# Attention with negated scores: one pass per head over local and context scores, value halves summed by TensorE

## Chip, cores and metric

One core of one Trainium2 chip runs the whole program. The metric is the device time of one execution in microseconds (us), the median over the runs shown. Engines: TensorE (PE, its weight loads PEld), VectorE (DVE), ScalarE (ACT), GpSimd (POOL), and SyncE (SP), which issues most DMAs.

## The reference, cut to the attention

The program is two transformer blocks on 1024 tokens of width 1024. The change lies in the attention of the first block. Half of the heads ("a", 8 heads on 2 key heads, with a sink column) look at a window of three 128-token blocks, the others ("b", 8 heads) at a neighbourhood with a learned bias; all look at 256 context tokens as well.

```
s_loc = einsum(q, k_local) * scale        # + bias for b
s_loc = where(mask, s_loc, -inf)
s_ctx = einsum(q, k_ctx) * scale
p = softmax(concat([s_loc, s_ctx, sink_col]))   # sink only for a
o = p_loc @ v_local + p_ctx @ v_ctx
```

## The kernel before, in words

The attention runs over 64 units: 32 of kind a, then 32 of kind b. A unit `(kind, i, p)` is one block of 128 queries (`i` = 0 to 7) and one pair of heads (`p` = 0 to 3; the two heads are `e` = 0, 1). A unit has three local key tiles of 128 (two where `i` is 0 or 7) and two context tiles, so 640 or 512 scores per query and head. Products are made exact to nearly fp32 by splitting one operand into a high and a low part in the type `fp32r`, so that a unit's scores take two matmuls for each piece (`z` = 0, 1), and its values are stacked with their low parts ("halves"), which have to be added at the end.

The steps of a unit `x`:

- `f_s(x, e)`: TensorE writes local scores into a tile `ps_l` (a PSUM bank, two of them) and context scores into `ps_c` (one bank for both heads).
- `f_max(x, e)`: VectorE reads `ps_l`, adds mask or bias, writes `sp` in SBUF and leaves the row maximum in `m` (one custom instruction and one that reads the accumulator). `f_maxc(x)`: the same for the context scores of both heads, with a column of zeros as addend, then the maximum of the two maxima (line 964) and its negation (line 968 for a, with the sink; line 971 for b).
- `f_exp(x, e)`: ScalarE computes the exponential with the negated maximum as bias, and the row sum.
- `f_pt(x, gi)`, `gi` = 0, 1, 2: TensorE transposes up to four 128x128 blocks of `sp` into a tile `pp` (a PSUM bank, three in rotation). For `gi` = 0 (the context blocks) ScalarE copies to `pf` and POOL makes high part (line 1003, a multiplication by ones) and low part (line 1004). For `gi` = 1, 2 ScalarE makes the high part (line 1006) and VectorE the low part (line 1007) straight from `pp`.
- `f_pv(x, part)`: the product with the values; ScalarE copies the result to `oT`.
- `f_fin(x)`: TensorE transposes the 128x128 blocks of `oT` (two for a, four for b) into a bank of their own (`otp`), and VectorE's reduction (line 1043) adds the halves while it copies to `O`.

The order is written by hand. Every engine takes its instructions in program order; there is no scheduler. Iteration `n` of the loop issues, in this order:

```
f_s(n,0) f_max(n,0)  f_exp(n-1,0)  f_pt(n-2,0)
f_s(n,1) f_max(n,1)  f_maxc(n)     f_exp(n-1,1)  f_pt(n-2,1)
f_pv(n-3,0)  f_pt(n-2,2)  f_pv(n-3,1)  f_fin(n-4)
conv_q(n//2+1) if n is even, then extra[n]
```

`conv_q` turns the queries of two units (four transposes into a `pp` tile, split by ScalarE, line 898, and VectorE, line 899). `extra[n]` holds work for later: the next head pair's keys (`b_k`, through `pp`), values (`b_v`, POOL) and bias (`b_bias`, one plain fp32 matmul into `pp` and six VectorE additions), the row sums (`a_end`, `b_end`), and splits of coming weights (`W.tick`).

Of the kernel before, what the change touches and what calls it, by code (L numbers as in the profile page):

```python
# [9 lines left out]
F32 = mybir.dt.float32  # L10
# [8 lines left out]
P = 128  # L19
# [193 lines left out]
def kernel(ctx: ExitStack, tc: tile.TileContext, a: dict, out: bass.AP, dbg=None):  # L213
# [219 lines left out]
    for i in (0, 2):  # L433
        nc.gpsimd.tensor_scalar(out=qg[:, i, :], in0=qg[:, i, :], scalar1=0.125, scalar2=None, op0=ALU.mult)
    nc.gpsimd.tensor_scalar(out=nsink, in0=sink, scalar1=-1.0, scalar2=None, op0=ALU.mult)
# [417 lines left out]
    maskA = wk.tile([P, 384], F32, name="maskA")  # L853
    maskB = wk.tile([P, 16, 24], F32, name="maskB")
# [53 lines left out]

    def addend(u, e):
        i = u[1]  # L910
        if u[0] == "a":
            return maskA[:, (128 if i == 0 else 0):(256 if i == 7 else 384)]
        p = u[2]
        if i == 0:
            return B["bE", p][:, e, 1:3].rearrange("p s r c -> p (s r c)")
        if i == 7:
            return B["bE", p][:, e, 0:2].rearrange("p s r c -> p (s r c)")
        return B["bI", p][:, e].rearrange("p s r c -> p (s r c)")

# [11 lines left out]
    def f_s(x, e):  # L931
        u = units[x]
        kk = kt(u[1])
        nl = len(kk) * P
        if e == 0:
            st["c", x] = ps_c.tile([P, 512], F32, tag="sc", name="ps_c", bufs=1)
        pc = st["c", x]
        pl = ps_l.tile([P, 512], F32, tag="sl", name="ps_l", bufs=2)
        k = k_stack(u, e)
        for z in range(2):  # L940
            q = qhl[x // 2][z][:, 2 * (x % 2) + e]
            nc.tensor.matmul(pl[:, 0:nl], q, k[:, kk[0] * P:kk[0] * P + nl], start=(z == 0), stop=(z == 1))
            nc.tensor.matmul(pc[:, e * 256:e * 256 + 256], q, k[:, 1024:1280], start=(z == 0), stop=(z == 1))
        st["l", x, e] = pl

    def f_max(x, e):
        u = units[x]
        if e == 0:
            st["sp", x] = wk.tile([P, 2, 640], F32, tag="sp", name="sp", bufs=3)
            st["m", x] = wk.tile([P, 8], F32, tag="m", name="m", bufs=4)  # L950
        nl = len(kt(u[1])) * P
        nc.vector.tensor_tensor_reduce(
            out=st["sp", x][:, e, 0:nl], in0=st.pop(("l", x, e))[:, 0:nl], in1=addend(u, e), scale=1.0, scalar=NEG,
            op0=ALU.add, op1=ALU.max, accum_out=st["m", x][:, e:e + 1])

    def f_maxc(x):
        u = units[x]
        nl = len(kt(u[1])) * P
        sp, m, pc = st["sp", x], st.pop(("m", x)), st.pop(("c", x))
        for e in range(2):  # L960
# [4 lines left out]
        nm, sm = stat(u)  # L965
        if u[0] == "a":
            h0 = 2 * u[2]
# [4 lines left out]
        st["nm", x] = (nm, sm)  # L972

    def f_exp(x, e):
        u = units[x]
        nm, sm = st["nm", x]
        sp = st["sp", x]
        w = len(kt(u[1])) * P + 256
        nc.scalar.activation(out=sp[:, e, :w], in_=sp[:, e, :w], func=AF.Exp, bias=nm[:, e:e + 1],
                             accum_out=sm[:, e:e + 1])  # L980

    def f_pt(x, gi):
        u = units[x]
        nk = len(kt(u[1])) + 2
        nl = nk - 2
# [12 lines left out]
        ph, pl = pt[:, g[0]:g[0] + len(g), 0, :], pt[:, g[0]:g[0] + len(g), 1, :]  # L998
        pv = pp[:, :w].rearrange("p (b t) -> p b t", t=P)
        if gi == 0:  # L1000
            pf = wk.tile([P, 4, P], F32, tag="pf", name="pf", bufs=2)
            nc.scalar.activation(out=pf, in_=pv, func=AF.Copy)
            nc.gpsimd.tensor_tensor(out=ph, in0=pf, in1=ones.unsqueeze(1).broadcast_to([P, 4, P]), op=ALU.mult)
            nc.gpsimd.tensor_tensor(out=pl, in0=pf, in1=ph.bitcast(F32), op=ALU.subtract)
        else:
            nc.scalar.activation(out=ph, in_=pv, func=AF.Copy)
            nc.vector.tensor_tensor(out=pl, in0=pv, in1=ph.bitcast(F32), op=ALU.subtract)

    def f_pv(x, part):
        u = units[x]  # L1010
        tiles = kt(u[1]) + [8, 9]
        nt_ = len(tiles)
        pt = st["pt", x]
# [3 lines left out]
        if u[0] == "a":  # L1017
            for j in (range(nt_ - 2) if part == 0 else range(nt_ - 2, nt_)):
                for z in range(2):
                    nc.tensor.matmul(po[:, 0:256], v_stack(u, 0, tiles[j]), pt[:, 2 * j:2 * j + 2, z, :],  # L1020
                                     start=(j == 0 and z == 0), stop=(j == nt_ - 1 and z == 1))
        else:
            e = part
            for j, tt in enumerate(tiles):
                nc.tensor.matmul(po[:, e * 256:e * 256 + 256], v_stack(u, e, tt),
# [8 lines left out]

    def f_fin(x):
        kind, i, p = units[x]
        oT = st.pop(("oT", x))
        nb = 2 if kind == "a" else 4
        po = ps_q.tile([P, 512], F32, tag="tq", name="otp")
        for j in range(nb):  # L1040
            tr(po[:, j * P:(j + 1) * P], oT[:, j * P:(j + 1) * P], ident)
        od = O[0 if kind == "a" else 1][:, i, p * 128:p * 128 + 128].rearrange("p (h d) -> p h d", d=64)
# [66 lines left out]
    def b_bias(p, e):  # L1109
        if e == 0:  # L1110
            B["bI", p] = BP[p % 2].tile([P, 2, 3, 16, 8], F32, tag="bI", name="bI")
            B["bE", p] = BP[p % 2].tile([P, 2, 3, 16, 8], F32, tag="bE", name="bE")
# [51 lines left out]
    for t, n in ((maskB, "mask_b"), (maskR, "mask_r"), (jrev, "jrev")):  # L1164
        nc.sync.dma_start(out=t, in_=a[n])
    maskP = wk.tile([P, 2, 640], F32, tag="sp", name="maskP", bufs=3)[:, 0, 0:384]
    load_natural(maskP, a["mask_a"])
    nc.gpsimd.tensor_copy(out=maskA.rearrange("p (b s c) -> p b s c", s=8, c=8),
                          in_=maskP.rearrange("p (b c s) -> p b s c", s=8, c=8))
    for g0 in (8, 0, 4):  # L1170
# [7 lines left out]
    for n in range(NU + 5):  # L1178
# [9 lines left out]
        if ok(n):  # L1188
            f_s(n, 1)
            f_max(n, 1)  # L1190
            f_maxc(n)
        if ok(n - 1):
# [1008 lines left out]
```

## Time and profile before

| what | value |
|---|---|
| median of 3 runs | 2707.81 us (2707.66 to 2713.16) |
| the profiled execution's own time | 2706.59 us |
| its span in the trace | 2704.8 us |
| mean granted clock of TensorE | 0.989 of full |
| busy over the whole span | PE 2569.5 us (95%), DVE 1713.1 (63%), ACT 1060.6 (39%), POOL 1187.3 (44%) |
| first and last of VectorE's score passes | 318.0 us and 638.1 us from the span's start |

The shares of the whole span are means over stages with different limits; the attention is about an eighth of it, and has to be read by itself. The time of a PE row is longer than the distance to the next row, since matmuls overlap; busy time of the weight loads (PEld) is nearer to the time in which TensorE really had work.

### The profile page before, as it was taken

Reading aid. Unit: us, or ns where it says so; the run is one execution under the profiler, and the core shown is the slowest. Engines: PE = TensorE matmul, PEld = TensorE weight load, DVE = VectorE, ACT = ScalarE, POOL = GpSimd, SP = SyncE. Lnnn points to the kernel's source line nnn. Section 1 sums busy time; section 2 is a strip of 40 time slices with the busy share of each in tenths; the row PEclk is TensorE's granted clock in tenths of the full one; section 3 lists DMA queues with packets and bytes.
Section 4 is the critical chain, followed back from the end, with each engine's and each line's share of the span. In section 5 each row is a group of like instructions: output and inputs, shape, how many; then the busy total and the mean of one; then the engine's idle time right before and its main releaser. Section 6 shows DMA issues by size and latency. Waiting matters only on the chain. (4 is left out here: it accounts for less than half of the span.)

```text
span 2704.8 us, 37053 instructions
## 1 busy us (share of the span) xinstructions
PE 2569.5 (95%) x13861; PEld 2135.2 (79%) x13861; DVE 1713.1 (63%) x3361; ACT 1060.6 (39%) x2613; POOL 1187.3 (44%) x1071
## 2 busy tenths in 40 slices
PE   7999888888989999999999999999999999999998
PEld 3999887778977888888878878877777777777786
DVE  4688699997276555555564532421777777777766
ACT  4644487776132222222223533322433333333333
POOL 2355266675256666666653221112333333333321
PEclk9999999999999999999999999999999999999999
DMA  6166421322111111111111111110111111111112
GB/s 241 32 191 205 139 52 34 87 52 87 32 40 32 62 48 47 47 47 48 62 52 51 50 35 44 32 47 32 40 47 47 47 47 47 47 47 47 47 47 86
DMA packets 152541, 170.86 MB, mean 63 GB/s; under 512 B 39444, under 2 KB 135460, under 8 KB 151336
## 3 DMA queue, kind: packets, MB, share of 16 engines
q1 hardware_dynamic: 152200, 168.35, 19.6%
q8 instruction: 109, 1.79, 0.3%
q0 software_dynamic: 160, 0.14, 0.1%
q14 instruction: 72, 0.59, 0.1%
HBM read 154.81 MB, written 13.65 MB: 62 GB/s over the span
## 5 line engine op out<-in xcount | busy, mean ns | idle before, releaser
L140 POOL TENSOR_TENSOR wlo<-raw,whi 128x512 fp32r<-128x512 f32 x132 | 179.2, 1362 | 448.2 <-ACT whi L139 419.3
L1656 PE MATMUL pgu<-h,whi 128*128 128x512 f32 x864 | 342.5, 396 | 3.1 <-DVE h L1592 3.1
L1657 PE MATMUL pgu<-h,wlo 128*128 128x512 f32 x864 | 341.2, 395 | 0.5 <-POOL wlo L140 0.5
L1655 PE MATMUL pgu<-h,whi 128*128 128x512 f32 x864 | 341.3, 395 | 0.0
L140 DVE TENSOR_TENSOR wlo<-raw,whi 128x512 fp32r<-128x512 f32 (+2 forms) x304 | 229.6, 768 | 154.0 <-ACT whi L139 153.3
L139 ACT ACTIVATE whi<-raw 128x512 fp32r<-128x512 f32 (+1 forms) x436 | 232.5, 552 | 173.0 <-DMA raw<-in_w_down 61.1
L1674 DVE TENSOR_TENSOR uv<-pgu,uv 128x512 f32<-128x512 f32 x216 | 148.4, 687 | 149.5 <-PE pgu L1657 128.2
L237 PE MATMUL pdn<-wlo,hid 128*128 128x512 f32 x576 | 227.3, 395 | 12.5 <-DVE wlo L140 12.5
L236 PE MATMUL pdn<-whi,hid 128*128 128x512 f32 x576 | 226.4, 393 | 1.4 <-DVE uv L1383 1.1
L238 PE MATMUL pdn<-whi,hid 128*128 128x512 f32 x576 | 226.6, 393 | 0.0
L1384 POOL TENSOR_TENSOR x<-x,uv 128x512 f32<-128x512 f32 x144 | 192.2, 1359 | 31.5 <-DVE uv L1383 28.6
L1656 PEld LDWEIGHTS pgu<-h,whi 128*128 128x128 f32 x864 | 162.2, 188 | 42.3 <-DVE h L1592 3.6
L1655 PEld LDWEIGHTS pgu<-h,whi 128*128 128x128 f32 x864 | 162.5, 188 | 40.1
L1657 PEld LDWEIGHTS pgu<-h,wlo 128*128 128x128 f32 x864 | 162.2, 188 | 39.9 <-POOL wlo L140 0.9
L1525 POOL TENSOR_TENSOR hid<-sg,hid 128x512 fp32r<-128x512 f32 x80 | 107.1, 1343 | 193.6 <-ACT hid L1524 191.5
L1677 POOL TENSOR_TENSOR uv<-uv 128x512 f32<-128x512 f32 x72 | 106.7, 1481 | 163.6 <-DVE uv L1674 163.6
L236 PE MATMUL pin<-whi,h 128*128 128x256 f32 x512 | 146.1, 285 | 5.8 <-ACT hsq L634 2.1
L237 PE MATMUL pin<-wlo,h 128*128 128x256 f32 x512 | 146.1, 285 | 1.7 <-DVE wlo L140 1.7
L238 PE MATMUL pin<-whi,h 128*128 128x256 f32 x512 | 146.1, 285 | 0.2 <-DVE h L706 0.2
L237 PEld LDWEIGHTS pdn<-wlo,hid 128*128 128x128 f32 x576 | 108.1, 188 | 42.0 <-DVE wlo L140 17.6
L1524 ACT ACTIVATE hid<-sg 128x512 fp32r<-128x512 f32 x80 | 50.3, 632 | 231.6 <-DVE sg L1522 231.6
L236 PEld LDWEIGHTS pdn<-whi,hid 128*128 128x128 f32 x576 | 108.2, 188 | 27.9 <-DVE uv L1383 1.5
(387 smaller groups left out, 7101.7 us busy)
## 6 DMA issues: line engine op xcount, KB each, us to landing
raw<-in_ffn_w_up SPq DMA_DIRECT2D x22, 1024.0 KB
mraw<-in_w_mod SPq DMA_DIRECT2D x32, 512.0 KB
raw<-in_w_gate SPq DMA_DIRECT2D x11, 1024.0 KB
raw<-in_w_up SPq DMA_DIRECT2D x11, 1024.0 KB
raw<-in_w_down SPq DMA_DIRECT2D x11, 1024.0 KB
raw<-in_ffn_w_down SPq DMA_DIRECT2D x11, 1024.0 KB
raw<-in_w_in SPq DMA_DIRECT2D x9, 1024.0 KB
wm<-in_w_mod SPq DMA_DIRECT2D x8, 1024.0 KB
```

The lines of the kernel that those rows point to most:

```text
L139: nc.scalar.activation(out=hi, in_=src, func=AF.Copy)
L140: (engine or self.engine or nc.vector).tensor_tensor(out=lo, in0=src, in1=hi.bitcast(F32), op=ALU.subtract)
L236: nc.tensor.matmul(ps, lh, rh, start=(i == 0), stop=False)
L237: nc.tensor.matmul(ps, lh, rl, start=False, stop=False)
L238: nc.tensor.matmul(ps, ll, rh, start=False, stop=(i == n - 1))
L1384: nc.gpsimd.tensor_tensor(out=xs, in0=xs, in1=tmp, op=ALU.add)
L1525: nc.gpsimd.tensor_tensor(out=hl[:, c], in0=sg[:, cc, c], in1=hh[:, c].bitcast(F32), op=ALU.subtract)
L1655: nc.tensor.matmul(ps, lh, rh, start=start and k == 0, stop=False)
L1656: nc.tensor.matmul(ps, lh, rl, start=False, stop=False)
L1657: nc.tensor.matmul(ps, ll, rh, start=False, stop=stop and k == n - 1)
L1674: nc.vector.tensor_tensor(out=o, in0=ps, in1=u, op=ALU.add)
L1677: nc.gpsimd.tensor_tensor(out=o, in0=u, in1=v, op=ALU.add)
```

## The change

1. The query gains are scaled by -0.125 instead of 0.125, and mask, bias matrix and bias masks are negated once, at the start of the stage (four small POOL instructions and a memset there). All scores are then negated, and the least of them is the bias that `f_exp` needs; `f_exp` takes `scale=-1.0`.
2. Local and context scores of a head lie side by side in one tile `ps_s` of two banks (two tiles, so four banks). `maskA` grows to 896 columns (zeros, mask, zeros), the bias `bI` to 1024 (bias of head 0, zeros, bias of head 1), so that one instruction can add over all 640 scores and leave the least. `f_maxc` is gone. The starting value of the minimum is the negated sink for a (a column read per partition). Only the units of b with `i` = 0 or 7 keep two passes, the second starting from the first's result.
3. For some units context comes ahead of local (`order`). The `pp` groups of `f_pt` are now the tiles in order, so POOL's share (`gi` = 0) is the first four blocks instead of the context blocks.
4. `f_fin` adds the halves by matmuls with `twice`, an identity of 64 columns over an identity of 64 columns (two plain fp32 matmuls of 64 columns for a, four for b), into a `pp` tile; the bank of `otp` is gone. VectorE only copies 128x128.
5. POOL's two multiplications by ones become `tensor_copy`.

```
-    ps_l = pool("ps_l", space=PSUM, stack=st_ps)
-    ps_c = pool("ps_c", space=PSUM, stack=st_ps)
+    ps_s = pool("ps_s", space=PSUM, stack=st_ps)
...
-    ps_q = pool("ps_q", space=PSUM, stack=st_ps)
...
+        ps = ps_s.tile([P, 1024], F32, tag="s", name="ps_s", bufs=2)[:, a0:a0 + w]
+        lo, co = (256, 0) if c1 else (0, nl)
...
+            nc.tensor.matmul(ps[:, lo:lo + nl], q, k[:, kk[0] * P:kk[0] * P + nl], start=(z == 0), stop=(z == 1))
+            nc.tensor.matmul(ps[:, co:co + 256], q, k[:, 1024:1280], start=(z == 0), stop=(z == 1))
...
+        at0 = nsink[:, 2 * u[2] + e:2 * u[2] + e + 1] if u[0] == "a" else -NEG
+        for c0, n, in1 in addends(u, e):
             nc.vector.tensor_tensor_reduce(
-                out=sp[:, e, nl:nl + 256], in0=pc[:, e * 256:e * 256 + 256], in1=zeros, scale=1.0, scalar=NEG,
-                op0=ALU.add, op1=ALU.max, accum_out=m[:, 2 + e:3 + e])
-        nc.vector.tensor_tensor(out=m[:, 4:6], in0=m[:, 0:2], in1=m[:, 2:4], op=ALU.max)
...
-            nc.vector.scalar_tensor_tensor(out=nm, in0=m[:, 4:6], scalar=-1.0, in1=nsink[:, h0:h0 + 2],
-                                           op0=ALU.mult, op1=ALU.min)
-        else:
-            nc.vector.tensor_scalar(out=nm, in0=m[:, 4:6], scalar1=-1.0, scalar2=None, op0=ALU.mult)
+                out=st["sp", x][:, e, c0:c0 + n], in0=ps[:, c0:c0 + n], in1=in1, scale=1.0, scalar=at0,
+                op0=ALU.add, op1=ALU.min, accum_out=nm)
+            at0 = nm
...
-        g = [list(range(2 * nl, 2 * nk)), list(range(0, 4)), list(range(4, 2 * nl))][gi]
+        g = list(range(4 * gi, min(4 * gi + 4, 2 * nk)))
...
-            nc.gpsimd.tensor_tensor(out=ph, in0=pf, in1=ones.unsqueeze(1).broadcast_to([P, 4, P]), op=ALU.mult)
+            nc.gpsimd.tensor_copy(out=ph, in_=pf)
...
-        nb = 2 if kind == "a" else 4
-        po = ps_q.tile([P, 512], F32, tag="tq", name="otp")
-        for j in range(nb):
-            tr(po[:, j * P:(j + 1) * P], oT[:, j * P:(j + 1) * P], ident)
...
-        nc.vector.tensor_reduce(
-            out=od, in_=po[:, :nb * P].rearrange("p (h x d) -> p h d x", h=2, d=64), axis=AX.X, op=ALU.add)
+        nb = 1 if kind == "a" else 2
+        po = pp_tile()
+        for e in range(2):
+            for j in range(nb):
+                b = (nb * e + j) * P
+                nc.tensor.matmul(po[:, e * 64:e * 64 + 64], oT[:, b:b + P], twice, start=(j == 0), stop=(j == nb - 1))
+        nc.vector.tensor_copy(out=O[0 if kind == "a" else 1][:, i, p * 128:p * 128 + 128], in_=po[:, 0:128])
```

What it does to the order of two engines is seen best in one unit. VectorE in an a unit with three local tiles, from its score passes to the last step of `f_fin`, before (`ISA` with 128x1 is the read of the accumulator; `stat` holds the negated maximum):

```order
L952 ISA sp,m<-ps_l,maskA 128x384 [waits PE_49]
L952 ISA m 128x1
L952 ISA sp,m<-ps_l,maskA 128x384 [waits PE_49]
L952 ISA m 128x1
L961 ISA sp,m<-ps_c,zero_3969 128x256 [waits PE_49]
L961 ISA m 128x1
L961 ISA sp,m<-ps_c,zero_3969 128x256
L961 ISA m 128x1
L964 TENSOR_TENSOR m<-m 128x2 [waits DVE_49]
L968 SCALAR_TENSOR_TENSOR stat<-m,nsink 128x2 [waits DVE_49]
L1007 TENSOR_TENSOR pt<-pp,pt 128x4x128 [waits Activation_49,Pool_49]
L1043 TENSOR_REDUCE o_3966<-otp 128x128 [waits PE_49]
```

and of the change:

```order
L961 ISA sp,stat<-ps_s,maskA,nsink 128x640 [waits PE_49]
L961 ISA stat 128x1
L961 ISA sp,stat<-ps_s,maskA,nsink 128x640 [waits PE_49]
L961 ISA stat 128x1
L998 TENSOR_TENSOR pt<-pp,pt 128x4x128 [waits Activation_49,Pool_49]
L998 TENSOR_TENSOR pt<-pp,pt 128x2x128 [waits Activation_49]
L1036 COPY o_3966<-pp 128x128 [waits PE_49]
```

Four passes became two, the two small instructions are gone, and the first low-part subtraction follows the passes directly. TensorE in an a unit, from the second group of transposes to the next unit's scores, before:

```order
L241 MATMUL pp<-ident,sp 128x128 [waits DVE_49]
L241 MATMUL pp<-ident,sp 128x128 x3
L1020 MATMUL po<-pt,VA 128x256 [waits Activation_49]
L1020 MATMUL po<-pt,VA 128x256 x5
L241 MATMUL pp<-ident,sp 128x128 [waits Activation_49]
L241 MATMUL pp<-ident,sp 128x128
L1020 MATMUL po<-pt,VA 128x256 [waits Pool_49] x2
L1020 MATMUL po<-pt,VA 128x256 x2
L241 MATMUL otp<-ident,oT 128x128 x2
L942 MATMUL ps_l<-kstA_4001,q_5648 128x384 [waits DVE_49]
```

and of the change:

```order
L241 MATMUL pp<-ident,sp 128x128 [waits DVE_49]
L241 MATMUL pp<-ident,sp 128x128 x3
L1011 MATMUL po<-pt,VA 128x256 [waits Activation_49,Pool_49]
L1011 MATMUL po<-pt,VA 128x256 [waits Pool_49]
L1011 MATMUL po<-pt,VA 128x256 x4
L241 MATMUL pp<-ident,sp 128x128 [waits Activation_49]
L241 MATMUL pp<-ident,sp 128x128
L1011 MATMUL po<-pt,VA 128x256 x4
L1035 MATMUL pp<-twice,oT 128x64 [waits DVE_49]
L1035 MATMUL pp<-twice,oT 128x64
L948 MATMUL ps_s<-kstA_3995,q_5363 128x384 [waits DVE_49]
```

The wait for POOL moved from the second part of the value product to its start, and the last step of a unit now waits for VectorE to have emptied a `pp` tile.

## Rows read from the trace of the kernel before

**Rows 1.** Busy time by stretch: most of the a units, most of the b units
```profile
core 0: us, PE busy (x) PEld busy (x) DVE busy (x) ACT busy (x) POOL busy (x), PEclk, DMA share, GB/s
...
335.00:465.00 130.00, 111.21 (x851) 104.09 (x852) 126.32 (x403) 104.84 (x255) 81.94 (x69) 0.99 0.18 42
...
475.00:640.00 165.00, 138.22 (x1023) 125.97 (x1022) 158.37 (x477) 124.10 (x274) 114.33 (x108) 0.97 0.22 54
```

**Rows 2.** Groups of PE in the two stretches: four of these matmuls make a unit
```profile
L943 PE MATMUL ps_c<-kstA,q 128*128 128x256 f32 x104 | 29.6, 288 | 1.6 <-DVE m L961 1.6
...
L943 PE MATMUL ps_c<-kstB,q 128*128 128x256 f32 x118 | 34.3, 296 | 1.2 <-DVE m L961 0.9
```

**Rows 3.** Waits from 318 to 650 us: who waited for whom, us in total, times, longest
```profile
PEld pp L241 <- DVE pt L1007: 38.6, 40, 3.0
```

**Rows 4.** Groups of VectorE, whole span: count, then busy us, mean ns, idle before
```profile
L964 DVE TENSOR_TENSOR m<-m 128x2 f32<-128x2 f32 x64 | 39.5, 617 | 2.2
...
L1043 DVE TENSOR_REDUCE o<-otp 128x128 f32<-128x512 f32 x32 | 21.7, 679 | 2.5 <-PE otp L241 2.5
...
L971 DVE TENSOR_SCALAR bstat<-m 128x2 f32<-128x2 f32 x32 | 15.8, 495 | 1.1
L1043 DVE TENSOR_REDUCE o<-otp 128x128 f32<-128x256 f32 x32 | 13.2, 413 | 0.0
L968 DVE SCALAR_TENSOR_TENSOR stat<-m,nsink 128x2 f32<-128x2 f32 x32 | 12.9, 402 | 1.1
```

**Rows 5.** Timeline of VectorE in one a unit: start us, us
```profile
424.33 0.55 DVE L952 CUSTOM_DVE_ANT_0 sp<-ps_l,maskA 128x384 f32<-128x384 f32 x1
...
424.81 0.42 DVE L961 CUSTOM_DVE_ANT_0 sp<-ps_c,zero 128x256 f32<-128x256 f32 x1
...
425.16 0.42 DVE L961 CUSTOM_DVE_ANT_0 sp<-ps_c,zero 128x256 f32<-128x256 f32 x1
425.50 0.08 DVE L961 DVE_READ_ACCUMULATOR2_ANT m<- 128x1 f32 x1
425.62 1.08 DVE L964 TENSOR_TENSOR m<-m 128x2 f32<-128x2 f32 x1
```

**Rows 6.** Timeline of POOL at the same time
```profile
425.41 1.28 POOL L1004 TENSOR_TENSOR pt<-pf,pt 128x512 fp32r<-128x512 f32 x1
```

**Rows 7.** Groups of VectorE and POOL, whole span: nearest rows to the new operations
```profile
L439 DVE COPY vec<-vtp 128x128 f32<-128x128 f32 x2 | 0.6, 292 | 3.8 <-PE vtp L241 3.8
...
L2027 DVE SCALAR_TENSOR_TENSOR sp<-sp,eg,pu 128x256 f32<-128x256 f32 x60 | 28.8, 479 | 69.7 <-PE pu L2019 66.3
...
L1003 POOL TENSOR_TENSOR pt<-pf,ones 128x512 fp32r<-128x512 f32 x64 | 82.8, 1293 | 83.8 <-ACT pf L1002 83.8
```

**Rows 8.** Timeline of weight loads: those of one bias matmul in plain fp32
```profile
598.02 0.30 PEld L1114 LDWEIGHTS pp<-braw,jrev 128*128 128x128 f32 x2 [1.73 <-DVE pt L1007]
```

**Rows 9.** Timeline of PE, one b unit: the tiles that pp and otp take
```profile
547.64 0.66 PE L241 MATMUL pp<-ident,sp 128*128 128x128 f32 x4 [1.14 <-DVE pt L1007]
...
548.74 0.60 PE L241 MATMUL pp<-ident,sp 128*128 128x128 f32 x4
...
549.77 0.38 PE L241 MATMUL pp<-ident,sp 128*128 128x128 f32 x2
...
550.58 0.60 PE L241 MATMUL otp<-ident,oT 128*128 128x128 f32 x4
551.02 0.60 PE L241 MATMUL pp<-ident,qraw 128*128 128x128 f32 x4
```

**Rows 10.** Timeline of ACT and VectorE, same unit: what frees these tiles
```profile
548.42 0.60 ACT L1002 ACTIVATE pf<-pp 128x512 f32<-128x512 f32 x1 [0.47 <-PE pp L241]
...
552.38 1.01 DVE L1007 TENSOR_TENSOR pt<-pp,pt 128x512 fp32r<-128x512 f32 x2
553.31 0.68 DVE L1043 TENSOR_REDUCE o<-otp 128x128 f32<-128x512 f32 x1
553.91 0.68 DVE L899 TENSOR_TENSOR q<-pp,q 128x512 fp32r<-128x512 f32 x1
```

More of the change, by code (lines that the diff above doesn't have):

```diff
@@ L852 @@
     b0 = pool("attn_b0", "left", stack=st_wk)
-    maskA = wk.tile([P, 384], F32, name="maskA")
+    maskA = wk.tile([P, 896], F32, name="maskA")
+    twice = wk.tile([P, 64], F32, name="twice")
     maskB = wk.tile([P, 16, 24], F32, name="maskB")
@@ L907, in v_stack, with order, addends @@
         return VA[:, tt, u[2] // 2, :] if u[0] == "a" else B["v", u[2]][:, tt, e, :]
-    def addend(u, e):
-        i = u[1]
-        if u[0] == "a":
[L912 to L918, printed above, removed]
+    def order(u, e):
+        kk = kt(u[1])
+        first = u[1] == 7 if u[0] == "a" else 0 < u[1] < 7 and e == 1
+        return [8, 9] + kk if first else kk + [8, 9]
+    def addends(u, e):
+        i, p, nl = u[1], u[2], len(kt(u[1])) * P
+        if u[0] == "a":
+            a0 = 384 if i == 0 else 0 if i == 7 else 256
+            return [(0, nl + 256, maskA[:, a0:a0 + nl + 256])]
+        if i in (0, 7):
+            ed = B["bE", p][:, e, (1 if i == 0 else 0):(3 if i == 0 else 2)].rearrange("p s r c -> p (s r c)")
+            return [(0, nl, ed), (nl, 256, zeros)]
+        return [(0, 640, B["bI", p][:, 0:640] if e == 0 else B["bI", p][:, 384:1024])]
     def stat(u):
@@ L934, in f_s @@
         nl = len(kk) * P
[L935 to L938, printed above, removed]
+        c1 = order(u, e)[0] == 8
+        w = nl + 256
+        a0 = 512 - (256 if c1 else nl)
+        ps = ps_s.tile([P, 1024], F32, tag="s", name="ps_s", bufs=2)[:, a0:a0 + w]
+        lo, co = (256, 0) if c1 else (0, nl)
         k = k_stack(u, e)
@@ L941, in f_s @@
             q = qhl[x // 2][z][:, 2 * (x % 2) + e]
-            nc.tensor.matmul(pl[:, 0:nl], q, k[:, kk[0] * P:kk[0] * P + nl], start=(z == 0), stop=(z == 1))
-            nc.tensor.matmul(pc[:, e * 256:e * 256 + 256], q, k[:, 1024:1280], start=(z == 0), stop=(z == 1))
-        st["l", x, e] = pl
+            nc.tensor.matmul(ps[:, lo:lo + nl], q, k[:, kk[0] * P:kk[0] * P + nl], start=(z == 0), stop=(z == 1))
+            nc.tensor.matmul(ps[:, co:co + 256], q, k[:, 1024:1280], start=(z == 0), stop=(z == 1))
+        st["s", x, e] = ps
     def f_max(x, e):
@@ L949, in f_max @@
             st["sp", x] = wk.tile([P, 2, 640], F32, tag="sp", name="sp", bufs=3)
[L950 to L960, printed above, removed]
-            nc.vector.tensor_tensor_reduce(
-                out=sp[:, e, nl:nl + 256], in0=pc[:, e * 256:e * 256 + 256], in1=zeros, scale=1.0, scalar=NEG,
-                op0=ALU.add, op1=ALU.max, accum_out=m[:, 2 + e:3 + e])
-        nc.vector.tensor_tensor(out=m[:, 4:6], in0=m[:, 0:2], in1=m[:, 2:4], op=ALU.max)
-        nm, sm = stat(u)
-        if u[0] == "a":
-            h0 = 2 * u[2]
-            nc.vector.scalar_tensor_tensor(out=nm, in0=m[:, 4:6], scalar=-1.0, in1=nsink[:, h0:h0 + 2],
-                                           op0=ALU.mult, op1=ALU.min)
-        else:
-            nc.vector.tensor_scalar(out=nm, in0=m[:, 4:6], scalar1=-1.0, scalar2=None, op0=ALU.mult)
-        st["nm", x] = (nm, sm)
+            st["nm", x] = stat(u)
+        ps, nm = st.pop(("s", x, e)), st["nm", x][0][:, e:e + 1]
+        at0 = nsink[:, 2 * u[2] + e:2 * u[2] + e + 1] if u[0] == "a" else -NEG
+        for c0, n, in1 in addends(u, e):
+            nc.vector.tensor_tensor_reduce(
+                out=st["sp", x][:, e, c0:c0 + n], in0=ps[:, c0:c0 + n], in1=in1, scale=1.0, scalar=at0,
+                op0=ALU.add, op1=ALU.min, accum_out=nm)
+            at0 = nm
     def f_exp(x, e):
@@ L978, in f_exp @@
         w = len(kt(u[1])) * P + 256
-        nc.scalar.activation(out=sp[:, e, :w], in_=sp[:, e, :w], func=AF.Exp, bias=nm[:, e:e + 1],
+        nc.scalar.activation(out=sp[:, e, :w], in_=sp[:, e, :w], func=AF.Exp, bias=nm[:, e:e + 1], scale=-1.0,
                              accum_out=sm[:, e:e + 1])
@@ L984, in f_pt @@
         nk = len(kt(u[1])) + 2
-        nl = nk - 2
         if gi == 0:
@@ L1010, in f_pv @@
         u = units[x]
-        tiles = kt(u[1]) + [8, 9]
-        nt_ = len(tiles)
+        tiles = [order(u, e) for e in range(2)]
+        nt_ = len(tiles[0])
         pt = st["pt", x]
@@ L1019, in f_pv @@
                 for z in range(2):
-                    nc.tensor.matmul(po[:, 0:256], v_stack(u, 0, tiles[j]), pt[:, 2 * j:2 * j + 2, z, :],
+                    nc.tensor.matmul(po[:, 0:256], v_stack(u, 0, tiles[0][j]), pt[:, 2 * j:2 * j + 2, z, :],
                                      start=(j == 0 and z == 0), stop=(j == nt_ - 1 and z == 1))
@@ L1023, in f_pv @@
             e = part
-            for j, tt in enumerate(tiles):
+            for j, tt in enumerate(tiles[e]):
                 nc.tensor.matmul(po[:, e * 256:e * 256 + 256], v_stack(u, e, tt),
@@ L1110, in b_bias @@
         if e == 0:
-            B["bI", p] = BP[p % 2].tile([P, 2, 3, 16, 8], F32, tag="bI", name="bI")
+            B["bI", p] = BP[p % 2].tile([P, 1024], F32, tag="bI", name="bI")
+            nc.gpsimd.memset(B["bI", p][:, 384:640], 0.0)
             B["bE", p] = BP[p % 2].tile([P, 2, 3, 16, 8], F32, tag="bE", name="bE")
@@ L1165 @@
         nc.sync.dma_start(out=t, in_=a[n])
+    for t in (maskB.rearrange("p r c -> p (r c)"), maskR, jrev):
+        nc.gpsimd.tensor_scalar(out=t, in0=t, scalar1=-1.0, scalar2=None, op0=ALU.mult)
+    nc.vector.tensor_copy(out=twice, in_=ident[:, 0:64])
+    nc.vector.tensor_tensor(out=twice, in0=twice, in1=ident[:, 64:128], op=ALU.add)
+    nc.gpsimd.memset(maskA, 0.0)
     maskP = wk.tile([P, 2, 640], F32, tag="sp", name="maskP", bufs=3)[:, 0, 0:384]
     load_natural(maskP, a["mask_a"])
-    nc.gpsimd.tensor_copy(out=maskA.rearrange("p (b s c) -> p b s c", s=8, c=8),
-                          in_=maskP.rearrange("p (b c s) -> p b s c", s=8, c=8))
+    nc.gpsimd.tensor_scalar(out=maskA[:, 256:640].rearrange("p (b s c) -> p b s c", s=8, c=8),
+                            in0=maskP.rearrange("p (b c s) -> p b s c", s=8, c=8),
+                            scalar1=-1.0, scalar2=None, op0=ALU.mult)
     for g0 in (8, 0, 4):
@@ L1190 @@
             f_max(n, 1)
-            f_maxc(n)
         if ok(n - 1):
```

10 lines of the change are left out of this document (5 added, 5 removed).

## The prediction, made before the changed kernel ran

> **What bounds the kernel now.** First the busy time by stretch. The attention takes some 320 us, and in its two long stretches VectorE is busy 126.32 of 130 us (97%) and 158.37 of 165 us (96%) [rows 1]. The reader should see that no other engine is near that: TensorE's weight loads, which follow TensorE's real work better than its matmul rows, take 104.09 us (80%) and 125.97 us (76%), ScalarE 104.84 and 124.10 us, POOL 63% and 69%. TensorE's granted clock is 0.99 and 0.97, so the clock is no large term here.
>
> Second, how many units these stretches hold. A unit has four context-score matmuls, so 104 rows are 26 a units and 118 rows are 29.5 b units [rows 2]: 130/26 = 5.00 us for an a unit, 165/29.5 = 5.59 us for a b unit. Per unit VectorE is busy 4.86 and 5.37 us, weight loads 4.00 and 4.27 us, ScalarE 4.03 and 4.21 us.
>
> Third, the waits. The longest that TensorE has is for a low-part subtraction of VectorE, 38.6 us in 40 times [rows 3]: a `pp` tile was not free because VectorE came late. So the pace of the stage is VectorE's, and less work there shortens the stage, until the next engine binds. TensorE and ScalarE are both close behind, at about 4.0 to 4.3 us a unit. That caps the gain, whatever VectorE saves.
>
> **The change, part by part.**
>
> *Score passes.* In the timeline a pass over 384 columns starts 0.48 us before the next instruction (424.33 to 424.81), one over 256 starts 0.35 us before (424.81 to 425.16) [rows 5]. The difference of 0.13 us for 128 columns is 1.04 ns per column, so a pass over 640 takes 0.48 + 256 x 1.04 ns = 0.75 us. Four passes cost 2 x 0.48 + 2 x 0.35 = 1.66 us, two merged ones 1.50: 0.16 us saved per unit. This is little; what is saved is the fixed part of two instructions. No row shows a pass that crosses two PSUM banks, or one with a start value per partition. Bounds: nothing for either; for the column, the nearest row is a VectorE instruction with such a scalar over 256 columns from PSUM, 479 ns [rows 7] against the 0.42 us of a pass over 256 [rows 5], 0.06 us dearer. I take 0.06 for each of the two passes of an a unit, and nothing for the banks; the far end for the banks, the double per column, is the first rival.
>
> *The two small instructions.* The maximum of maxima costs 617 ns, its negation 402 ns for a and 495 ns for b [rows 4], although they work on two columns. One instance shows why: it began at 425.62 and took 1.08 us [rows 5], to 426.70, and POOL's low part ran from 425.41 to 426.69 [rows 6]. It stood still until POOL was done. Both go, and the new passes read only one tensor from SBUF, as the old passes did, which ran beside POOL unhindered. Saved: 1.02 us (a), 1.11 us (b).
>
> *The last step.* The reduction costs 413 ns (a) or 679 ns (b) [rows 4]. A copy of 128x128 from PSUM takes 292 ns [rows 7]: 0.12 and 0.39 us saved.
>
> VectorE's sum per unit: a 0.16 - 0.12 + 1.02 + 0.12 = 1.18 us, b 0.16 + 1.11 + 0.39 = 1.66 us. It falls from 4.86 to 3.68 us and from 5.37 to 3.71 us. It is then below TensorE and ScalarE, so these savings can't all come out. If they did, 32 x 1.18 + 32 x 1.66 = 91 us would be the gain.
>
> *TensorE.* The transposes of `oT` are two or four instructions at 0.11 us each (550.58 to 551.02 for four) [rows 9]. In their place come as many matmuls of 64 columns, in plain fp32. The trace shows a plain fp32 matmul as two instructions with a weight load each: two loads within 0.30 us for a bias matmul [rows 8]. So the new step has four (a) or eight (b) instructions, each with the weight load of a transpose. Bounds: no dearer than now, if 64 columns instead of 128 halve each; or the 0.11 us of a transpose each, which adds 0.22 and 0.44 us. I take the middle, since half of the columns is spared and the load is not: 0.10 and 0.20 us. TensorE's floor is then 4.00 + 0.10 = 4.10 us (a) and 4.27 + 0.20 = 4.47 us (b).
>
> The Trainium skill says in "TensorE: Matmul & The Clock Gate", section Terms, that this chip's transpose mode is four times faster for fp32. By that, 64 plain columns cost what 256 transposed ones do, twice the present step; no row here shows a plain fp32 matmul of 64 columns. It would give the upper bound above.
>
> *The `pp` tiles.* `otp` gives up its bank, and its tile joins the three `pp` banks: 4.5 tiles per unit instead of 3.5. If VectorE goes as late as now, the tiles of one b unit are held as follows, from the first transposes to the end of the instruction that frees them [rows 9, 10]: 547.64 to 549.02 (1.38 us), 548.74 and 549.77 to at latest 553.39 (4.65 and 3.62), the last step's 550.58 to 553.99 (3.41), the query tile 551.02 to 554.59 (3.57, in every other unit, so 1.79). Together 14.85 us, over three banks 4.95 us per unit. This is already below 5.59, and four of these five holds contain the wait for VectorE's passes and small instructions, which get 1.66 us shorter. So the three banks don't set the pace, but they leave little slack.
>
> *POOL.* A copy instead of a multiplication: between nothing and the 1.29 us of that multiplication [rows 7], so never dearer. POOL is at most 69% busy, and its part is now needed at the start of the value product instead of near the end, most of a microsecond earlier; it was issued a whole unit before. I cost both at nothing. The four negations and the memset at the start stand ahead of the mask in POOL's queue, once: five times 1.29 us at most, nothing if they run while the mask is still under way. I take 1 us. The zeros in the bias tile, four times, cost POOL nothing that is waited for. On SP nothing is added.
>
> **The sum.** TensorE binds next, with ScalarE 0.1 to 0.3 us behind. Two engines that hand work to each other don't reach the 96 to 97% of VectorE alone; I take 93%. The pace is 4.10/0.93 = 4.41 us and 4.47/0.93 = 4.81 us. Gain: 32 x (5.00 - 4.41) + 32 x (5.59 - 4.81) = 18.9 + 25.0 = 44 us, less 1 us at the start: 43 us. The profiled execution took 2706.59 us, so 2663.6; the median of the runs is 1.2 us above that execution. Forecast: **2665 us**.
>
> **Rivals.**
>
> 1. *The merged pass is dear.* If it took two times 1.04 ns per column (two banks, or the start value), it would cost 0.08 + 640 x 2.08 ns = 1.41 us, 1.32 us more per unit, and VectorE would stay the bound at 5.00 (a) and 5.03 us (b), at 96% 5.21 and 5.24 us: 32 x 0.21 lost, 32 x 0.35 gained, 4 us faster, 2703 us, which is no change by the bound below. For it: no row shows such a pass. Against: the old passes over 256 and 384 differ by 1.04 ns per column and no more. It begins to bind where VectorE passes TensorE, at 0.96 us (a) or 1.13 us (b) per pass.
>
> 2. *Three banks for 4.5 tiles set the pace, and the kernel gets slower.* If the tile of the last step is freed late, each of the 3.5 tiles that VectorE frees waits behind one more merged pass, 0.75 us: 14.85 + 2.6 = 17.5 us of holds, 5.8 us per unit. Taken for both halves (only b's rows stand here): 32 x 0.8 + 32 x 0.2 = 32 us lost, 2740 us. It decides from holds of three times the present pace, 15.0 us (a) and 16.8 us (b). For it: TensorE waits for `pp` tiles even now [rows 3]. Against: the copy stands ahead of the next unit's passes in VectorE's order, and VectorE has over 1 us to spare.
>
> 3. *The plain matmuls cost their upper bound.* TensorE's floor is 4.22 and 4.71 us, the pace 4.54 and 5.06 us, the gain 32 x 0.46 + 32 x 0.53 = 32 us less 1: 2677 us. For it: each is two instructions with a full weight load. Against: half of the columns.
>
> 4. *VectorE's whole saving comes out:* 91 us, 2617 us. It needs TensorE and ScalarE to go below their present busy time of 4.0 us, which nothing in the change brings.
>
> **How the numbers follow.** Forecast 57%, rival 3 25%, rival 1 7%, rival 2 8%, rival 4 3%. The low end of the range is TensorE at 97% with no dearer last step: 4.12 and 4.40 us, a gain of 28 + 38 = 66 us, about 2641. The high end is TensorE at 87% with the upper bound of that step: 4.85 and 5.41 us, a gain of 11 us, about 2697; with rivals 1, 2 and 4 (18%) outside I close it at 2695. Anything within 0.2% (5.4 us) is about what a measurement of this kernel can't tell from no change. Faster by more: forecast, rivals 3 and 4, 85%. Within: rival 1, 7%. Slower: rival 2, 8%.
>
> **What would show it.** Right: VectorE's busy share in the attention falls to 75 to 85%, a merged pass row reads about 0.8 us with its successor 0.75 us later, and TensorE's weight loads rise to about 90% of the stage. The waits for VectorE's low part shrink to a few us, and the last score pass comes near 595 us instead of 638. The rows of the last step tell my middle from its bounds by their distance. Wrong: a pass row over 1 us (rival 1); TensorE still waiting tens of us for `pp` tiles while VectorE is idle (rival 2); or a stage that is shorter with a later stage that is longer, which nothing here foresees.

## The result, and the profile after

The changed kernel takes 2677.32 us (median of 4 runs, 2675.95 to 2680.64) against 2708.63 us before: ratio 0.988, interval 0.9868 to 0.9892, so 31 us faster. The forecast was 2665, the range 2641 to 2695. Below, a ratio stands for each kernel, to the kernel before on the same chip; 0.001 is 2.7 us, and an interval reaches 0.0012 to 0.0017 (3 to 5 us) to either side.

Busy time by stretch after, most of the a units and most of the b units, to be read against [rows 1]:

```profile
core 0: us, PE busy (x) PEld busy (x) DVE busy (x) ACT busy (x) POOL busy (x), PEclk, DMA share, GB/s
335.00:440.00 105.00, 99.45 (x786) 95.02 (x784) 85.64 (x211) 90.57 (x220) 54.87 (x63) 1.00 0.19 46
452.00:600.00 148.00, 140.00 (x1124) 134.26 (x1123) 114.44 (x321) 120.59 (x271) 90.79 (x111) 1.00 0.26 67
```

The context-score matmuls in the same two stretches give the units, as [rows 2] did (four matmuls a unit):

```profile
L949 PE MATMUL ps_s<-kstA,q 128*128 128x256 f32 x90 | 25.2, 281 | 0.0
...
L949 PE MATMUL ps_s<-kstB,q 128*128 128x256 f32 x120 | 33.1, 282 | 0.0
```

22.5 a units in 105 us are 4.67 us a unit (5.00 before), 30 b units in 148 us 4.93 us (5.59 before). VectorE, 97% and 96% busy before, is now at 82% and 77%; weight loads rose to 90.5% and 90.7%, ScalarE to 86% and 81%. VectorE is no longer the bound; TensorE is the busiest engine now, but idle for a tenth of the time. The granted clock is 1.00 in both stretches, against 0.99 and 0.97 before, where it was 0.85 on average from 500 to 525 us. VectorE, the bound there, was still busy for 23.06 of those 25 us, so by estimate at most some 2 us of the gain are the clock's.

Four of the longest waits (same columns as [rows 3], 318 to 620 us); the third is TensorE's longest:

```profile
DVE q L898 <- ACT q L897: 22.3, 28, 0.9
ACT q L897 <- PE pp L241: 21.9, 28, 1.7
PEld pp L241 <- DVE pt L998: 15.8, 28, 1.3
DVE pt L998 <- ACT pt L997: 14.2, 26, 2.6
```

The wait for VectorE's low part, 38.6 us in [rows 3], shrank to 15.8 and did not vanish. VectorE's new rows, groups of the a stretch and then of the b stretch:

```profile
L961 DVE CUSTOM_DVE_ANT_0 sp<-ps_s,maskA,nsink 128x640 f32<-128x640 f32 x44 | 37.1, 875 | 0.5
...
L961 DVE CUSTOM_DVE_ANT_0 sp<-ps_s,bI 128x640 f32<-128x640 f32 x46 | 36.2, 820 | 1.7 <-PE ps_s L949 1.3
...
L1036 DVE COPY o<-pp 128x128 f32<-128x128 f32 x30 | 8.5, 285 | 1.7 <-PE pp L1035 1.5
```

and two passes in the timeline of VectorE:

```profile
522.12 0.82 DVE L961 CUSTOM_DVE_ANT_0 sp<-ps_s,bI 128x640 f32<-128x640 f32 x1
522.87 0.08 DVE L961 DVE_READ_ACCUMULATOR2_ANT bstat<- 128x1 f32 x1
522.87 0.82 DVE L961 CUSTOM_DVE_ANT_0 sp<-ps_s,bI 128x640 f32<-128x640 f32 x1
```

The merged pass follows its like after 0.75 us, as worked out from [rows 5]; two banks cost nothing on top, the start value per partition 55 ns (875 against 820). Of the weight loads, the last step of one b unit:

```profile
528.63 0.98 PEld L1035 LDWEIGHTS pp<-twice,oT 128*128 128x128 f32 x8
529.48 0.48 PEld L241 LDWEIGHTS pp<-ident,qraw 128*128 128x128 f32 x4
```

Eight loads from 528.63 to 529.48 are 0.106 us each: the price of a transpose for each of the two instructions that a plain fp32 matmul is, the upper bound of the prediction.

Nothing moved outside the attention: the first score pass starts at 317.1 us (318.0 before), the last at 608.2 (638.1 before), and from there to the end it is 2066.0 us of the span of 2674.2, against 2066.7 before.

### The profile page after: what moved, and what is told of

The parts are those of the page before. It is cut to its first block, busy times and chain, and to the rows that moved or that the text cites. A ratio compares the mean times of both kernels' runs of the same rounds, so it can differ in the third digit from the quotient of the medians.

```text
span 2674.2 us, 37149 instructions
## 1 busy us (share of the span) xinstructions
PE 2575.6 (96%) x14053; PEld 2152.5 (80%) x14053; DVE 1631.4 (61%) x3011; ACT 1057.8 (40%) x2613; POOL 1139.3 (43%) x1079
```

## The experiments

Two things were to be settled: which part brings the 31 us, and why it is not more.

### The last step and POOL, alone and undone

**e1** puts the old last step into the change (transposes and reduction, in a `pp` tile); **e3** puts the new one into the kernel before, in its own bank.

```
-        nb = 1 if kind == "a" else 2
+        nb = 2 if kind == "a" else 4
...
+        for j in range(nb):
+            tr(po[:, j * P:(j + 1) * P], oT[:, j * P:(j + 1) * P], ident)
...
+        nc.vector.tensor_reduce(
+            out=od, in_=po[:, :nb * P].rearrange("p (h x d) -> p h d x", h=2, d=64), axis=AX.X, op=ALU.add)
```

> The changed kernel with the last step as before (two or four transposes and VectorE's reduction), but in a pp tile. Theory (TensorE is now the bound, and a plain fp32 matmul of 64 columns costs it two instructions of 0.106 us): TensorE gets 0.21 us (a) and 0.42 us (b) less per unit, 20 us in all, so 2657 us if nothing else binds; VectorE goes up by 0.13 and 0.39 us to about 3.9 and 4.2 us a unit and stands level with TensorE, so I expect 2660 to 2668 us. Rival (three pp banks set the pace): the tile of the last step is held 0.13 to 0.39 us longer, so 2677 to 2685 us.

> The kernel before with the new last step alone (plain fp32 matmuls, VectorE copies 128x128; its own PSUM bank stays). Theory (VectorE bounds the kernel before): VectorE loses 0.12 us (a) and 0.39 us (b) per unit, 16 us in all; TensorE gains 0.21 and 0.42 us, which its waits cover, so 2692 to 2698 us. Rival (the extra TensorE work delays the pp tiles as much): 2708 us or above.

Measured: e1 2673.75 us, 0.9863 (0.9848 to 0.9877); e3 2698.69 us, 0.9955 (0.994 to 0.997). So the new last step brings 12 us on the kernel before and costs some 5 us in the change, hardly more than the intervals: much less than TensorE's added time of 20 us (32 x 0.21 + 32 x 0.42). e1 lies between its theory and its rival, so neither account is complete; it gives back 20 us of TensorE's work, but also puts 17 us back on VectorE.

**e2** gives POOL its multiplications back in the change; **e4** makes only POOL's copies in the kernel before. Shown is e4's edit of the first of the two statements; e2's is the reverse.

```
-            nc.gpsimd.tensor_tensor(out=ph, in0=pf, in1=ones.unsqueeze(1).broadcast_to([P, 4, P]), op=ALU.mult)
+            nc.gpsimd.tensor_copy(out=ph, in_=pf)
```

> The changed kernel with POOL's two multiplications by ones back. Theory (POOL is not on the path): 0.68 us more POOL work per unit at 52 to 61% busy is covered, 2675 to 2680 us. Rival (the value product, which now starts with POOL's blocks, waits for POOL, and VectorE's low part waits for it too, 5.3 us already): 5 to 15 us slower, 2682 to 2692 us.

> The kernel before with POOL's copies in place of its multiplications, and nothing else. Theory (VectorE's two small instructions stand still while POOL runs): their mean of 1.02 to 1.11 us per unit falls by about 0.15 us as POOL is busy a fifth less, 10 us in all, 2698 us. Rival (they are slow by themselves): 2708 us, and the means stay at 617, 402 and 495 ns.

Measured: e2 2679.8 us, 0.9886 (0.9871 to 0.9901), no different from the change; e4 2685.7 us, 0.9906 (0.989 to 0.9923), so 25 us from POOL's copies alone, far more than expected. VectorE's groups of e4, to be read against [rows 4], show part of the way:

```profile
L964 DVE TENSOR_TENSOR m<-m 128x2 f32<-128x2 f32 x64 | 33.8, 528 | 2.2
...
L971 DVE TENSOR_SCALAR bstat<-m 128x2 f32<-128x2 f32 x32 | 12.7, 398 | 1.1
...
L968 DVE SCALAR_TENSOR_TENSOR stat<-m,nsink 128x2 f32<-128x2 f32 x32 | 9.9, 308 | 1.1
```

617, 495 and 402 ns became 528, 398 and 308, though nothing on VectorE was changed: POOL holds them up for less time. That is 12 us. Most of the rest is other VectorE instructions with two tensors from SBUF, 5 us together: the splits of weights (line 143, 769 ns before) and two steps of the row sums (lines 1050 and 1054, 354 and 244 ns before), here from 317 to 620 us of e4:

```profile
L143 DVE SCALAR_TENSOR_TENSOR wlo<-raw,vec,whi 128x256 fp32r<-128x256 f32 x8 | 3.6, 454 | 0.0
...
L1054 DVE TENSOR_TENSOR stat<-stat 128x8 f32<-128x8 f32 x8 | 1.2, 155 | 0.0
L1050 DVE TENSOR_TENSOR stat<-sink,stat 128x8 f32<-128x8 f32 x8 | 1.2, 155 | 0.0
```

The profiled execution of e4 is its slowest, 2690.22 us, 16 us below the profiled one of the kernel before, so these 17 us cover what that trace can show.

### The merged pass alone, and TensorE relieved

**e5** is the change with POOL's multiplications and the old last step (both edits above), so that the merged pass on negated scores is left. **e6** is the change with transposes in the last step and a VectorE copy; the low halves of the values are left out.

```
-                nc.tensor.matmul(po[:, e * 64:e * 64 + 64], oT[:, b:b + P], twice, start=(j == 0), stop=(j == nb - 1))
+            tr(po[:, j * P:(j + 1) * P], oT[:, j * P:(j + 1) * P], ident)
...
+                              in_=po[:, 0:nb * P].rearrange("p (h x) -> p h x", h=2)[:, :, 0:64])
```

> The changed kernel without its two other parts: POOL multiplies again and the last step is transposes and VectorE's reduction (in a pp tile). What is left is the negation and the merged pass. Theory (VectorE's stand-still behind POOL was most of what there was to gain, and any remedy for it takes it): 2672 to 2680 us. Rival (the parts add up, and POOL's copies carry their 25 us in the change too): about 2700 us.

> The changed kernel with the old transposes in the last step, but VectorE only copies 128x128 as in the change: the low halves of the values are left out of the sum. TensorE gets 0.21 us (a) and 0.42 us (b) less per unit, VectorE nothing more. Theory 1 (TensorE alone sets the pace): 20 us faster than the change, 2657 us. Theory 2 (TensorE, ScalarE and VectorE set it together through the pp tiles): 3 to 9 us faster, 2668 to 2674 us.

Measured: e5 2675.34 us, 0.9878 (0.9862 to 0.9895): the merged pass alone (with the small instructions gone) brings all that the change brings, and the other two parts add nothing on top that the intervals show. e6 2672.36 us, 0.9869 (0.9854 to 0.9884): with TensorE's extra 20 us gone, and VectorE's copy kept, some 3 us come back, less than the intervals. So TensorE's time is not the whole reason why more did not come. Its waits say where the time went:

```profile
PEld pp L241 <- DVE pt L998: 28.2, 41, 1.6
```

15.8 us of waits for the low part in the change became 28.2: 12 of the 20 us that the matmuls no longer use, TensorE spends waiting for a `pp` tile.

**e7** tried the chain of the query tile, which leads the waits after: `conv_q` between `f_pv(n-3,0)` and `f_pt(n-2,2)`.

```
+        if n % 2 == 0:
+            conv_q(n // 2 + 1)
...
-        if n % 2 == 0:
-            conv_q(n // 2 + 1)
```

> The changed kernel with conv_q issued between the two parts of the value product instead of at the end of the iteration; no work is added or taken away. Theory 2 (in every even iteration the query tile waits for the first low-part subtraction, and ScalarE, VectorE and the next passes wait for the query tile in turn): the 22 us in which ScalarE waits for TensorE's query transposes and the 22 us in which VectorE waits for ScalarE's query copy shrink to a few, and the kernel is 5 to 12 us faster, 2665 to 2672 us. Theory 1 (TensorE's work sets the pace): 2675 to 2679 us.

Measured: 2678.28 us, 0.9889 (0.9874 to 0.9904), no change. The wait only changed its place: now the last step's matmuls wait for VectorE's low part (10.8 us in the groups of weight loads), where the query tile's transposes did. Another order in the rotation of the same three banks doesn't help.

### The stand-still itself

**e9** leaves the kernel before as it is, POOL too, and writes only the small VectorE instructions in forms with one SBUF tensor and one output column (or a reduction).

```
-        nc.vector.tensor_tensor(out=m[:, 4:6], in0=m[:, 0:2], in1=m[:, 2:4], op=ALU.max)
+        nc.vector.tensor_reduce(out=m[:, 4:6], in_=m[:, 0:4].rearrange("p (s e) -> p e s", e=2), axis=AX.X, op=ALU.max)
...
-            nc.vector.scalar_tensor_tensor(out=nm, in0=m[:, 4:6], scalar=-1.0, in1=nsink[:, h0:h0 + 2],
-                                           op0=ALU.mult, op1=ALU.min)
+            for e in range(2):
+                nc.vector.tensor_scalar(out=nm[:, e:e + 1], in0=m[:, 4 + e:5 + e], scalar1=-1.0,
+                                        scalar2=nsink[:, h0 + e:h0 + e + 1], op0=ALU.mult, op1=ALU.min)
...
-            nc.vector.tensor_scalar(out=nm, in0=m[:, 4:6], scalar1=-1.0, scalar2=None, op0=ALU.mult)
+            for e in range(2):
+                nc.vector.tensor_scalar(out=nm[:, e:e + 1], in0=m[:, 4 + e:5 + e], scalar1=-1.0, scalar2=None, op0=ALU.mult)
```

> The kernel before with its two small VectorE instructions in forms that read a single tensor from SBUF: the maximum of maxima as a reduction, the negation as two instructions of one column (with the sink as a column scalar for a). POOL and everything else stay. Theory (the small instructions stand still behind POOL because they read two tensors, or one through both ports): each now takes 0.15 to 0.2 us, about 0.5 us per unit is saved, 32 us if VectorE stayed the bound, less as TensorE comes near: 2678 to 2690 us. Rival (small instructions behind a custom pass are slow by themselves): their sum stays above 1 us and the time at 2708 us or above, as there is one instruction more.

Measured: 2667.98 us, 0.985 (0.9835 to 0.9864): 41 us faster than before, with an instruction more, and 8 us better than the whole change. Its groups of VectorE, and its timeline in an a unit:

```profile
L969 DVE TENSOR_SCALAR stat<-m,nsink 128x1 f32<-128x1 f32 x64 | 10.7, 209 | 1.1
L964 DVE TENSOR_REDUCE m<-m 128x2 f32<-128x4 f32 x64 | 10.1, 158 | 2.2
...
L973 DVE TENSOR_SCALAR bstat<-m 128x1 f32<-128x1 f32 x64 | 6.9, 149 | 1.1
```

```profile
428.12 0.16 DVE L964 TENSOR_REDUCE m<-m 128x2 f32<-128x4 f32 x1
428.32 0.34 DVE L969 TENSOR_SCALAR stat<-m,nsink 128x1 f32<-128x1 f32 x2
428.57 1.01 DVE L1009 TENSOR_TENSOR pt<-pp,pt 128x512 fp32r<-128x512 f32 x2
```

and POOL's at the same time:

```profile
427.68 1.26 POOL L1006 TENSOR_TENSOR pt<-pf,pt 128x512 fp32r<-128x512 f32 x1
```

This is the place of [rows 5, 6] again, with POOL in the same instruction until 428.94: what took 1.08 us there takes 0.16 here, and the low part starts while POOL is still at work. All 64 instances of line 964, least, median and longest time in ns, before and then in e9:

```profile
L964 DVE TENSOR_TENSOR m<-m x64: 160/600/1285, 319.5 to 638.5; 128x2 f32<-128x2 f32 x64
```

```profile
L964 DVE TENSOR_REDUCE m<-m x64: 157/157/159, 319.5 to 598.2; 128x2 f32<-128x4 f32 x64
```

The old form takes 160 ns too when it is let: in the kernel before, the 9 instances that began while POOL was idle took 0.16 us each, of the 55 others 49 ended within 0.1 us of POOL's instruction, and 6, which began just as one of POOL's began or ended, took 0.16 us again. The cost of the two small instructions was waiting for POOL, not work. The Trainium skill says in "SBUF — State Buffer", section Terms, that VectorE and GpSimd arbitrate for a shared pair of ports that is held for a whole instruction, and that the loser blocks rather than shares; these rows agree.

### The last step's bank

**e10** is e9 with POOL's copies. Three kernels are built on it: **e12** has the change's last step in the old bank, **e11** the same in a `pp` tile (as in the change, three banks), **e13** the old last step in a `pp` tile, with four banks in the rotation. Shown is the line in which e11 differs from e12, and e13 from e10; e13 also raises the number of `pp` banks to 4.

```
-        po = ps_q.tile([P, 512], F32, tag="tq", name="otp")
+        po = pp_tile()
```

> The kernel before with the small VectorE instructions in one-input forms (measured alone at 2668 us) and now also POOL's copies instead of multiplications. Theory 1, that VectorE's standing still behind POOL was the loss and both remedies cure the same loss: within 4 us of 2668, although the copies alone brought 25 us on the kernel before. Theory 2, that POOL's time counts by itself (its results late, or other VectorE instructions slowed): 15 us or more below 2668, so at most 2653.

> The kernel before with one-input forms, POOL copies and the change's last step, in the bank that the last step had before. VectorE is spared 0.12 us (a) and 0.39 us (b) per unit, TensorE gets 0.21 and 0.42 us more. If VectorE is still the bound: 32 x 0.13 + 32 x 0.41 = 17 us below the kernel with one-input forms and copies. If TensorE binds by its weight loads at 93%: 4.44 and 5.02 us per unit, some 6 us above it.

> The kernel before with one-input forms, POOL copies and the change's last step, its tile in the rotation of three pp banks as in the change (the fourth bank is left unused). To be read against the same kernel with a bank of its own for that tile. Theory 1, that giving up the bank is what kept the change from its forecast: 6 to 10 us slower than with the bank of its own. Theory 2, that the bank costs nothing, as the prediction had it: within 2.5 us of it.

> The kernel before with one-input forms and POOL copies, its last step as before (transposes, reduction), with the last step's bank given to the rotation of pp: four banks for 4.5 tiles per unit instead of three for 3.5 and one apart. If the number of banks per tile sets the pace (1.17 tiles per bank before, 1.13 here): the same or up to 3 us faster. If what matters is that the last step does not stand in the rotation, between the tiles that ScalarE and VectorE free: 3 us slower or more.

| kernel | last step | its tile | us | ratio (interval) |
|---|---|---|---|---|
| e10 | transposes, reduction | bank of its own | 2665.74 | 0.9836 (0.9822 to 0.9851) |
| e13 | transposes, reduction | one of four `pp` banks | 2666.06 | 0.9834 (0.9817 to 0.985) |
| e12 | `twice` matmuls, copy | bank of its own | 2673.4 | 0.9867 (0.9852 to 0.9881) |
| e11 | `twice` matmuls, copy | one of three `pp` banks | 2686.3 | 0.9913 (0.9898 to 0.9928) |

POOL's copies, worth 25 us alone, are worth 2 us beside the one-input forms (e10 against e9, within the intervals): two remedies for one loss. The dearer matmuls cost 8 us (e12 against e10); the same edit brought 12 us in e3. VectorE is not much less busy in e10 than in the kernel before (97% and 96% there):

```profile
335.00:440.00 105.00, 97.83 (x776) 93.80 (x775) 100.17 (x386) 94.56 (x232) 57.18 (x65) 1.00 0.20 49
452.00:590.00 138.00, 128.21 (x995) 120.62 (x994) 131.69 (x492) 118.32 (x266) 86.79 (x105) 0.99 0.29 71
```

That is 95% in both stretches. What has changed is TensorE: its weight loads are at 89% and 87% instead of 80% and 76%, so there is little room left for longer ones. The loss of the bank costs 13 us more (e11 against e12), and the last step's tile in the rotation costs nothing where the rotation has a fourth bank (e13). Weight loads of e11 in one b unit, with the query tile after the last step:

```profile
523.00 0.97 PEld L1045 LDWEIGHTS pp<-twice,oT 128*128 128x128 f32 x8
525.15 0.42 PEld L241 LDWEIGHTS pp<-ident,qraw 128*128 128x128 f32 x4 [1.17 <-DVE pt L1009]
```

VectorE of e11 at that time:

```profile
522.32 0.56 DVE L952 CUSTOM_DVE_ANT_0 sp<-ps_l,bI 128x384 f32<-128x384 f32 x1
...
524.41 1.01 DVE L1009 TENSOR_TENSOR pt<-pp,pt 128x512 fp32r<-128x512 f32 x2
```

and e12's weight loads at the like place:

```profile
524.87 0.97 PEld L1046 LDWEIGHTS otp<-twice,oT 128*128 128x128 f32 x8
525.70 0.48 PEld L241 LDWEIGHTS pp<-ident,qraw 128*128 128x128 f32 x4
```

In e11 the query tile needs the bank of the unit's second group of transposes, and gets it only when VectorE, which has its score passes first, has made that group's low part: TensorE stands still for 1.17 us. In e12 it goes on at once. All waits of weight loads for a `pp` tile that VectorE's low part holds come to 19.7 us in e11 and 7.0 in e12, which is the 13 us between the two. Does the change have this wait? The groups of weight loads for the query tile, 318 to 622 us, idle time before them at the end of the row, in e12, then e11, the change, and e6:

```profile
L241 PEld LDWEIGHTS pp<-ident,qraw 128*128 128x128 f32 x120 | 14.3, 155 | 0.0
```

```profile
L241 PEld LDWEIGHTS pp<-ident,qraw 128*128 128x128 f32 x120 | 13.3, 146 | 10.2 <-DVE pt L1009 10.2
```

```profile
L241 PEld LDWEIGHTS pp<-ident,qraw 128*128 128x128 f32 x120 | 13.6, 148 | 7.4 <-DVE pt L998 7.1
```

```profile
L241 PEld LDWEIGHTS pp<-ident,qraw 128*128 128x128 f32 x120 | 13.2, 142 | 14.4 <-DVE pt L998 14.4
```

It has. The kernel before and all whose last step has a bank of its own, or a fourth in the rotation, show 0.0 there; those with three banks 5 to 14.5 us, e7 apart, where the last step waits instead. What the bank costs in the change itself was not tried: its four score banks, three `pp` banks and one for `po` leave none. So the merged pass was never run without the loss of the bank, and what it would bring then is open. For e5 against e9 (0.9878 against 0.985, though e5 has less work on VectorE) the same cause is likely, with 12.5 us of this wait in e5 and none in e9, but not shown apart.

The fastest version run is e10, 2665.74 us, level with e13 and, within the intervals, with e9: it is the kernel before with three VectorE and two POOL statements rewritten, and 12 us faster than the change (0.9836 against 0.988).

## Why the prediction was right, and where it was off

The time lies in the range, 12 us above the forecast. Two of the signs named for it did not come: the waits for the low part shrank to 15.8 us instead of a few, and the last score pass came at 608.2 us instead of near 595. Point by point:

- *VectorE bounds, and the small instructions stand still behind POOL*: right, and it is nearly all of the gain. e9 takes away only that and brings 41 us; e4 and e5 reach the same loss from POOL's side and by deletion.
- *The merged pass*: 0.75 us to the next, banks free, start value 0.055 us instead of 0.06. Rival 1 falls. (0.13 us over 128 columns is 1.02 ns a column, not 1.04; it changes nothing here.)
- *The reduction becomes a copy*: 285 ns instead of the 292 used.
- VectorE's busy time per unit came to 85.64/22.5 = 3.81 and 114.44/30 = 3.81 us, against 3.68 and 3.71 forecast; where the 0.1 us comes from was not followed up.
- *TensorE's last step*: the middle was taken, the upper bound came. This term was mis-sized: 0.21 and 0.42 us per unit instead of 0.10 and 0.20. The reason for the middle, that half of the columns is spared, was wrong: an instruction of 64 columns costs 0.106 us, like a transpose of 128. The Trainium skill's rule that was named there ("TensorE: Matmul & The Clock Gate", section Terms) gave twice the old step, and e12's and the change's rows agree with that. Against e10, e12 measured 8 us for it.
- *The pp tiles, costed at nothing*: this is the step that failed. The tiles' holds were added up and divided by three banks, 4.95 us, less than the pace, and were expected to shrink; they did. Read in the same way, the two b units of the change whose first transposes start at 519.84 and 525.89 us have holds of about 11 and 8 us, 3.7 and 2.7 us per bank, well below the pace of 4.93, and still TensorE waits 15.8 us for such tiles in the stage. A mean over three banks hides where a rotation binds: at the query tile of every other unit, which stands right behind the last step's tile and needs the one bank that VectorE has not yet freed. Where it could be measured it cost 13 us (e11 against e12); in the change TensorE idles 7.4 us there.
- *93% for TensorE*: measured 90.5% and 90.7%. e12, the same last step with its own bank, has 97.45 of 105 us (93%) in the a units and 137.29 of 148 us (93%) in the b units, so the figure was fair without the waits for `pp` tiles.
- *What makes up the 12 us*, an estimate by the prediction's own sum: the weight loads of the change are 95.02/22.5 = 4.22 us (a) and 134.26/30 = 4.48 us (b), where 4.10 and 4.47 were forecast. At 93% these would be 4.54 and 4.81 us a unit; measured were 4.67 and 4.93. So about 4 us come from the last step, in the a units alone, and 8 us from the waits. The b units met the forecast's 4.47 us although their last step cost its upper bound: their other loads are shorter than before (for the values 189 ns instead of 193, for the scores 190 instead of 197 to 199), which goes with the clock of 1.00 instead of 0.97, and the stretch after has the last steps of some a units in it. How much each does was not taken apart.
- *POOL's copy, costed at nothing*: right in the change (e2), though it is worth 25 us by itself. The start cost nothing instead of 1 us.
- *Rival 3* named the measured time, 2677 us, and its price for the matmuls was right. But it made them the only reason, and e6, which takes them out, gives back only about 3 us: with three banks the wait takes their place. That its time came out is in part luck: its paces were 4.54 and 5.06 us, the measured ones 4.67 and 4.93, and the two errors cancel.
- *Rival 2* had the right mechanism with the wrong price and sign: the wait for a bank took away part of the gain, not all of it. VectorE's copy is not late, as the prediction said; what is late is the low part of the second group.

## What to carry to other kernels

Where a tiny VectorE instruction has a mean many times its work, look at what GpSimd does in that moment, and rewrite the instruction with one SBUF tensor before rebuilding the stage: here three rewritten statements brought more than the whole change. Before a tile moves into a shared rotation, don't stop at the banks' mean time per unit: look, in the unit that takes the most tiles, at which instruction frees the bank that the next tile needs. And an edit that shifts work from one engine to another can change its sign with the room that the second one has: the same matmuls brought 12 us while TensorE's weight loads were at 76 to 80%, and cost 8 when they were at 87 to 89%.

## What the runs showed of the hardware that was not expected

One-input forms of a two-column operation ran beside a GpSimd instruction in 149 to 209 ns, where the two-tensor forms, and the one-tensor form with two output columns (line 971), had means of 402 to 617 ns. A GpSimd copy of 128x512 is half as dear as the multiplication by ones, 1293 ns in [rows 7]; from POOL's groups of the change:

```profile
L994 POOL CAST pt<-pf 128x512 fp32r<-128x512 f32 x64 | 39.8, 622 | 105.7 <-ACT pf L993 105.5
```
